# Attention scores of a second dense stage: three products over 64 rows per head instead of two over 128 stacked rows

## The chip, the cores and the metric

One Trainium2 chip, one NeuronCore. The metric is the device time of one execution in microseconds (us), the median of several runs. TensorE (PE in the profile; PEld are its weight loads), VectorE (DVE), ScalarE (ACT), GpSimd (POOL) and SyncE (SP) work side by side, each through its own queue in order.

## The reference

Two transformer blocks on one sequence of 1024 tokens of 1024 features, each with a dense part and a mixture of 32 experts. The change lies in the dense part of the second block, which has two kinds of attention, 8 heads of 64 features each:

```python
h = _modulate(_rmsnorm(x, g_mix[layer]), shift_mix, scale_mix)
qkv = h @ w_in[layer]
...
o_dil = _dilated_mixture(heads_d(q_d), heads_d(k_d), heads_d(v_d)).reshape(b, s, D_DIL)
o_sb = _stick_breaking_attention(heads_s(q_s), heads_s(k_s), heads_s(v_s)).reshape(b, s, D_SB)
mixed = jnp.concatenate([_rmsnorm(o_dil, g_dil_out[layer]), _rmsnorm(o_sb, g_sb_out[layer])], axis=-1)
x = x + gate_mix[:, None, :] * (mixed @ w_out[layer])
```

In the first kind the scores `q @ k.T / 8` get a bias by distance and a softmax over all keys up to the query. In the second, `A[t,s] = sigmoid(z_ts) * prod_{s<j<t} (1 - sigmoid(z_tj))` with the same scores z. In both the weights then multiply the values.

## The kernel before

All is float32. Where precision matters, a product is made of exact parts: each operand is split into a high part (the leading 12 bits) and a low part, in a format that TensorE takes in one pass, and the products high x high, high x low and low x high are summed (`mm3`, lines 108 to 113).

The second dense stage is `dense2` (from line 1241). It norms the eight blocks of 128 tokens, and then works through eight jobs, pairs of heads: four of the first kind (`kind` 0), then four of the second. For each pair, `pair_qkv` (line 1328) makes keys, queries and values of 1024 tokens with `gemm` (line 284; 24 products of 512 columns for each half of the tokens and each of the three), and `pair` (line 1346) does the attention. `pair_qkv` of the next pair is issued after `pair` of this one. The order on each engine is set by a scheduler at build time, which interleaves them: dense products of the next pair lie between the scores, transposes and outputs of this pair. At run time each engine keeps to that order.

The keys and queries come out of `gemm` with the two heads in the two halves of the 128 partitions. `put_q` (line 302) writes for each head a tile `qs` of 128 partitions: 64 with the high part, 64 with the low part. `put_k` (line 312) writes for each head a tile `kh` that holds the high part twice and a tile `kl` that holds the low part twice; the second copy is made by GpSimd (line 321). So a head's scores are two products over all 128 rows, `qs` with `kh` and `qs` with `kl` (`scores`, line 335; lines 345 and 346). Keys up to the end of the query block are taken in one cut of up to 512, or in two equal cuts when there are more; a cut fills a PSUM buffer `sc`, of which there are three.

`pair` goes through eight blocks of 128 queries and in each through two heads `j`. Kind 0: VectorE adds the bias from a table `tb` and takes the maximum (line 1368), ScalarE takes the exponential, VectorE normalises into `s`. Kind 1: ScalarE takes the sigmoid into `be` (line 1380), GpSimd zeroes what lies after the query (line 1381), `ke` is one minus that, VectorE runs a product scan into `s` (line 1389) and multiplies. Then TensorE transposes the weights (`tp`, line 1399), ScalarE copies them to `pT`, and the output `po` takes both heads alternately in the two halves of its partitions (line 1404). That product has 64 columns of weights: a tile shape of 128 rows x 64 columns, against 128 x 128 for everything around it.

When the first kind is done, `half_out` (line 1300) multiplies its output with half of the output projection: for each of eight row blocks it loads rows of x into one of four buffers `xs`, makes 24 products, scales them into `ys` (VectorE, line 1324), adds (GpSimd, line 1325) and stores to `xp`. In the order its products fill the last pair. `xs` and `ys` take the places of the query and key tiles of the pairs with even number (`qs1`, `kh0`, `kh1`, `kl0`, `kl1`); the pairs with odd number hold theirs in another pool. After the stage `out_proj` (line 748) does the other half of the projection, the router and the experts.

```python
qs, kh, kl = ([new(2 * n + j, f"{m}{j}") for j in range(2)] for n, m in enumerate(("qs", "kh", "kl")))
vt = p.tile([P, NB, P], FT, name="vt", bufs=2)
...
for j in range(2):
    parts = self.scores(pp, qs[j], kh[j], kl[j], qb)
```

Of the kernel before, what the change touches and what calls it, by code (L numbers as in the profile page):

```python
# [8 lines left out]
FT = mybir.dt.float32  # L9
# [3 lines left out]
AF = mybir.ActivationFunctionType  # L13
OP = mybir.AluOpType
# [19 lines left out]
V_AT = 3  # L34
LATE = {1: (2, 3, 5), 2: (2, 3, 4, 5, 6, 7)}


def bcast(ap, n=P):
    """Rows of DRAM read into all partitions."""
    return bass.AP(tensor=ap.tensor, offset=ap.offset, ap=[[0, n]] + [list(a) for a in ap.ap])  # L40


def rev(ap):
    """A [partition, free] view read from its end."""
    step, n = ap.ap[-1]
    return bass.AP(tensor=ap.tensor, offset=ap.offset + step * (n - 1), ap=[list(ap.ap[0]), [-step, n]])
# [5 lines left out]
class Shared:  # L52
    """A pool of which some tags, two tiles each, lie in the tiles that are kept throughout."""
# [11 lines left out]
class Kern:  # L65
# [21 lines left out]
    def held(self, i, shape, dt, name):  # L87
        """One of six tiles of 4 KB that stay in place: weights, then rows of x, then queries and keys."""
        return self.keep.tile(shape, dt, tag=f"k{i}", name=name, bufs=1)

# [1 line left out]
    def later(self, op, first, why, sync=True):  # L92
        """op after the end of first, or, in one queue, after its issue."""
# [4 lines left out]
    def split(self, pool, src, shape, tag, bufs=None, eng=None):  # L98
        """Exact parts of float32: hi has the leading 12 bits, lo the rest."""
# [27 lines left out]
    def ada_first(self, which, p, pp, n):  # L127
        """Shift and scale of the first norm, features on partitions; the first step starts n loads."""
# [49 lines left out]
    def mod_store(self, which, p, r, ps):  # L178
        """Four rows of the modulation: with its bias; for a scale, gain * (1 + it). They go to DRAM,
        the first four (the first shift and scale) stay as sums."""  # L180
# [19 lines left out]
    def mod_cols0(self, which, pp, tag, bufs):  # L200
        """mod_first() from the sums of mod_store()."""
# [7 lines left out]
    def mod_first(self, which, sums):  # L209
        """Per feature (on partitions): scale and shift of the first norm."""  # L210
# [10 lines left out]
    def cond(self, which):  # L221
        """silu(c), features on partitions."""
# [39 lines left out]
    def mod_cols(self, which, pp, tag, j):  # L262
        """Per feature (on partitions): scale and shift from the modulation rows j + 1 and j."""
# [11 lines left out]
    def mod_row(self, pool, which, j, name, after=None, t=None):  # L275
        """Modulation row j on all partitions."""
# [7 lines left out]
    def gemm(self, pp, w, x, evac, halves=(0, 1), after=None):  # L284
        """evac(half, psum) with 128 output features on partitions, 512 tokens."""
# [16 lines left out]
    def put_q(self, qs, half, ps):  # L302
        """Two heads' queries, scaled; each stacked with its own low part."""
# [8 lines left out]
    def put_k(self, kh, kl, half, ps, after=None):  # L312
        """Two heads' keys: high parts, and low parts, each twice."""
# [11 lines left out]
    def put_v(self, pool, pp, vt, half, ps):  # L325
        """Two heads' values, tokens on partitions."""
# [8 lines left out]
    def scores(self, pp, qs, kh, kl, qb):  # L335
        """Scores of a block of queries with all keys up to it: (psum, first key, keys)."""
        nc = self.nc
        n = (qb + 1) * P
        cuts = [(0, n)] if n <= 512 else [(0, n // 2), (n // 2, n)]
        got = []  # L340
        for c0, c1 in cuts:
            sc = pp.tile([P, 512], FT, tag="sc", name="sc", bufs=3)
            o = sc[:, :c1 - c0]
            q = qs[:, qb * P:(qb + 1) * P]
            nc.tensor.matmul(o, q, kh[:, c0:c1], start=True, stop=False)
            nc.tensor.matmul(o, q, kl[:, c0:c1], start=False, stop=True)
            got.append((o, c0, c1 - c0))
        return got

# [1 line left out]
    def t5_flag(self, ahead):  # L351
        """Biases for positions that don't rise by one, where needed. Returns a register: 0, or 1
        where they were. ahead() starts the loads that needn't wait for it."""
# [1249 lines left out]
```

## Time and profile before

| | |
|---|---|
| time, median of 3 runs | 2549.51 us (2544.28 to 2554.2) |
| profiled execution: span from the first to the last instruction | 2542.7 us (its own time is not listed; 6.8 us less than the median of the runs) |
| busy share of the span: PE, DVE, ACT, POOL | 89%, 65%, 25%, 16% |
| second dense stage, first score to last output | 1318.7 to about 1892 us |
| output projection, router | about 1899 to 2000 us |
| experts of the second block | about 2000 to 2498 us |

The page of the profile gives one execution. Busy times count the time from an instruction's start to its end; on TensorE the next product starts well before the last one's end, so the distance of starts says more than the duration. Idle time is put down to what released the instruction after it; "issue" means that nothing the profile shows released it.

### The profile page before, as it was taken

To read this page: it belongs to the slowest core of one execution; us is meant where nothing else is said; L and a number is where in the kernel's file an instruction comes from. 1 tells how busy PE (TensorE), PEld (TensorE's weight loads), DVE (VectorE), ACT (ScalarE), POOL (GpSimd) and SP (SyncE) were. 2 spreads that over 40 slices of the span, in tenths; PEclk is the share of its full clock that TensorE was granted. 3 is DMA by queue.
4 is the path that set the end of the run, shared out by engine and by line. 5 is a ranking of instruction groups with operands and counts; after the bars stand their busy time and mean duration, and the time that the engine had idled before them with its cause. 6 is when DMAs were issued, how large, how long until landed. Compare 5 with 4: busy or idle time off the path is not lost. (4 is left out here: it accounts for less than half of the span.)

```text
span 2542.7 us, 55236 instructions
## 1 busy us (share of the span) xinstructions
PE 2258.6 (89%) x23070; PEld 1634.2 (64%) x23070; DVE 1664.2 (65%) x3712; ACT 646.3 (25%) x1406; POOL 415.1 (16%) x509
## 2 busy tenths in 40 slices
PE   7999999999969999979389999999989699999761
PEld 4777767687847655646267777777668476655530
DVE  4565678724787777766365555667868877776535
ACT  4455211111310000000155455555543100000001
POOL 2101012113220000000230100222342200000002
PEclk9999999999979999999689999999999799999986
DMA  7232477727569999998831111000547799999997
GB/s 275 84 96 63 137 264 242 240 74 261 193 253 424 424 422 423 381 414 365 356 124 55 34 50 34 26 30 18 179 165 292 279 424 423 423 418 382 426 424 291
DMA packets 112125, 628.38 MB, mean 247 GB/s; under 512 B 16025, under 2 KB 33018, under 8 KB 86522
## 3 DMA queue, kind: packets, MB, share of 16 engines
q1 hardware_dynamic: 92592, 574.96, 57.9%
q0 software_dynamic: 17312, 48.35, 4.9%
q8 instruction: 185, 3.03, 0.5%
q10 hardware_dynamic: 1962, 1.44, 0.2%
q14 instruction: 74, 0.61, 0.1%
HBM read 579.57 MB, written 55.61 MB: 250 GB/s over the span
## 5 line engine op out<-in xcount | busy, mean ns | idle before, releaser
L888 PE MATMUL ps<-gu,xT 128*32 128x256 f32 x10368 | 635.1, 389 | 51.2 <-DMA gu<-in_w_up_dram 37.8
L888 PEld LDWEIGHTS ps<-gu,xT 128*32 128x32 f32 x10368 | 392.6, 113 | 260.4 <-issue 69.5
L903 DVE TENSOR_TENSOR yq<-py,g 32x256 f32<-32x256 f32 x648 | 271.9, 420 | 176.0 <-PE py L899 131.6
L899 PE MATMUL py<-dn,hT 128*32 128x256 f32 x5184 | 332.4, 390 | 50.2 <-DVE hT L895 48.7
L110 PE MATMUL mm<-hh,gh 128*128 128x512 f32 x864 | 347.3, 403 | 4.8 <-ACT hh L1451 3.5
L111 PE MATMUL mm<-hl,gh 128*128 128x512 f32 x864 | 345.0, 399 | 0.4 <-DVE hl L1475 0.4
L112 PE MATMUL mm<-hh,gl 128*128 128x512 f32 x864 | 344.1, 398 | 0.0
L883 DVE STREAM_TRANSPOSE xT<-xg 32x256 f32<-32x256 f32 x648 | 282.1, 435 | 70.6 <-PE ps L888 60.0
L899 PEld LDWEIGHTS py<-dn,hT 128*32 128x32 f32 x5184 | 184.9, 112 | 164.0 <-DVE hT L895 82.1
L891 ACT ACTIVATE sg<-ps 128x128 f32<-128x128 f32 x162 | 44.7, 277 | 913.1 <-PE ps L888 905.0
L110 PEld LDWEIGHTS mm<-hh,gh 128*128 128x128 f32 x864 | 162.9, 189 | 48.1 <-ACT sg L517 5.2
L112 PEld LDWEIGHTS mm<-hh,gl 128*128 128x128 f32 x864 | 163.0, 189 | 37.0 <-issue 0.9
L111 PEld LDWEIGHTS mm<-hl,gh 128*128 128x128 f32 x864 | 163.2, 189 | 36.5 <-issue 1.0
L912 POOL DMA_INDIRECT s_y<-yq,sx x39 | 38.9, 996 | 606.9 <-DVE yq L903 564.5
L169 DVE SCALAR_TENSOR_TENSOR acc<-wa,cs,acc 128x512 f32<-128x512 f32 x140 | 110.1, 791 | 36.0 <-DMA wa<-in_w_ada_dram 33.2
L105 DVE TENSOR_TENSOR gl<-graw,gh 128x1024 fp32r<-128x1024 f32 x61 | 80.9, 1326 | 65.5 <-ACT gh L104 64.0
L104 ACT ACTIVATE gh<-graw 128x1024 fp32r<-128x1024 f32 x66 | 69.9, 1059 | 197.2 <-PE mm L111 176.7
L893 DVE TENSOR_TENSOR hm<-sg,ps 128x128 f32<-128x128 f32 x162 | 64.0, 396 | 74.7 <-ACT sg L891 70.2
L1400 ACT ACTIVATE pT<-tp 128x512 f32<-128x512 f32 (+2 forms) x192 | 90.1, 491 | 85.3 <-PE tp L1399 84.4
L1389 DVE TENSOR_TENSOR_SCAN s<-ke 128x128 f32<-128x128 f32 (+7 forms) x64 | 92.3, 1444 | 21.0 <-ACT ke L1385 19.8
L1404 PE MATMUL po<-pT,vt 128*64 128x128 f32 x1152 | 103.2, 282 | 1.9 <-ACT pT L1400 1.8
L1404 PEld LDWEIGHTS po<-pT,vt 128*64 128x64 f32 x1152 | 70.7, 136 | 38.3 <-issue 25.1
(377 smaller groups left out, 3220.8 us busy)
## 6 DMA issues: line engine op xcount, KB each, us to landing
gu<-in_w_gate_dram SPq DMA_DIRECT2D x62, 2048.0 KB, 18.7
gu<-in_w_up_dram SPq DMA_DIRECT2D x62, 2048.0 KB, 22.2
dn<-in_w_down_dram SPq DMA_DIRECT2D x62, 2048.0 KB, 23.6
wa<-in_w_ada_dram SPq DMA_DIRECT2D x96, 512.0 KB, 5.0
graw<-in_w_in_dram SPq DMA_DIRECT2D x54, 512.0 KB, 3.6
cy<-s_y SPq DMA_DIRECT2D x32, 512.0 KB, 6.7
bt<-s_t5all SPq DMA_DIRECT2D x32, 256.0 KB, 2.8
s_hp<-rh SPq DMA_DIRECT2D x16, 512.0 KB, 2.9
```

The lines of the kernel that those rows point to most:

```text
L105: (eng or nc.vector).tensor_sub(lo, src, hi.bitcast(FT))
L110: o = nc.tensor.matmul(ps, lh, rh, start=first, stop=False)
L111: nc.tensor.matmul(ps, lh, rl, start=False, stop=False)
L112: nc.tensor.matmul(ps, ll, rh, start=False, stop=last)
L169: nc.vector.scalar_tensor_tensor(acc, wt[:, k], c, acc, op0=OP.mult, op1=OP.add)
L883: turn = V.transpose(out=xT[32 * q:32 * q + 32].rearrange("p k t -> p (k t)"), in_=xg[o, 256 * q:256 * q + 256])
L888: mm = nc.tensor.matmul(ps[32 * q:32 * q + 32], xT[:, k, :], gu[:, :, k, q * P:(q + 1) * P], start=(k == 0), stop=(k == KD - 1))
L899: nc.tensor.matmul(py[32 * q:32 * q + 32], hT[:, k, :], dn[:, k, 256 * q:256 * q + 256], start=(k == 0), stop=(k == 3))
L903: V.tensor_mul(yq[o, 256 * q:256 * q + 256], py[r], g2[r])
L1389: V.tensor_tensor_scan(out=rev(s[:, :n]), data0=rev(ke[:, :n]), data1=rev(ke[:, :n]), initial=1.0, op0=OP.mult, op1=OP.bypass)
L1400: nc.scalar.activation(pT[:, 4 * g:4 * g + m], pt[:, :m], AF.Copy)
L1404: nc.tensor.matmul(po[64 * j:64 * j + 64, :], vt[:, kb, 64 * j:64 * j + 64], pTs[j][:, kb, :], start=(kb == 0), stop=(kb == qb))
```

## The change

The scores of the second dense stage are made of three products over the 64 rows of a head, high x high, low key, low query, for both heads in turn: head 0 in rows 0 to 63, head 1 in rows 64 to 127, each into a buffer `sc` of its own. Keys and queries are kept as four tiles of both heads (`qh`, `ql`, `kh`, `kl`), written by `put_parts` in full height; nothing is copied. `pair` takes the scores of both heads, cut by cut, before it goes on with each head. Buffers: `s` 4 instead of 3, `st` 6 instead of 3, the tag `u` (`tb`, `be`, `ke`) 5 instead of 4. `half_out` has fewer tiles to take over, so its fourth `xs` and its `ys` take the two tiles of `vt`. The order that kept the first pair's copies behind the norm goes with the copies. The first block's own attention (`sliding`) keeps `put_q` and `put_k`. The change also drops docstrings and comments; code lines move down by up to 14.

```diff
+    def put_parts(self, hi, lo, half, ps, scale=1.0):
+        nc = self.nc
+        s = slice(half * 512, half * 512 + 512)
+        nc.scalar.activation(hi[:, s], ps, AF.Copy, scale=scale)
+        nc.vector.scalar_tensor_tensor(lo[:, s], ps, scale, hi[:, s].bitcast(FT), op0=OP.mult, op1=OP.subtract)
+
-    def scores(self, pp, qs, kh, kl, qb):
+    def scores(self, pp, held, qb):
         nc = self.nc
+        qh, ql, kh, kl = held[:4]
         n = (qb + 1) * P
-        cuts = [(0, n)] if n <= 512 else [(0, n // 2), (n // 2, n)]
-        got = []
-        for c0, c1 in cuts:
-            sc = pp.tile([P, 512], FT, tag="sc", name="sc", bufs=3)
-            o = sc[:, :c1 - c0]
-            q = qs[:, qb * P:(qb + 1) * P]
-            nc.tensor.matmul(o, q, kh[:, c0:c1], start=True, stop=False)
-            nc.tensor.matmul(o, q, kl[:, c0:c1], start=False, stop=True)
-            got.append((o, c0, c1 - c0))
-        return got
+        t = slice(qb * P, (qb + 1) * P)
+        for c0, c1 in [(0, n)] if n <= 512 else [(0, n // 2), (n // 2, n)]:
+            sc = [pp.tile([P, 512], FT, tag="sc", name="sc", bufs=3)[:, :c1 - c0] for j in range(2)]
+            for m, (q, k) in enumerate(((qh, kh), (qh, kl), (ql, kh))):
+                for j in range(2):
+                    r = slice(64 * j, 64 * j + 64)
+                    nc.tensor.matmul(sc[j], q[r, t], k[r, c0:c1], start=(m == 0), stop=(m == 2))
+            yield c0, c1 - c0, sc
...
-        g1 = qp.tile([P, D], FT, tag="qs0", name="g1", bufs=1)
+        g1 = qp.tile([P, D], FT, tag="qh", name="g1", bufs=1)
...
-        xs = [qp.tile([P, D], FT, tag=t, name="xs", bufs=1) for t in ("qs1", "kh0", "kh1", "kl0")]
-        ys = qp.tile([P, 2, 512], FT, tag="kl1", name="ys", bufs=1)
+        xs = [qp.tile([P, D], FT, tag=t, name="xs", bufs=1) for t in ("ql", "kh", "kl")] + [qp.tile([P, D], FT, tag="vt", name="xs", bufs=2)]
+        ys = qp.tile([P, 2, 512], FT, tag="vt", name="ys", bufs=2)
...
-        qs, kh, kl = ([new(2 * n + j, f"{m}{j}") for j in range(2)] for n, m in enumerate(("qs", "kh", "kl")))
+        qh, ql, kh, kl = (new(n, m) for n, m in enumerate(("qh", "ql", "kh", "kl")))
...
-        puts = (lambda half, ps: self.put_k(kh, kl, half, ps, after),
-                lambda half, ps: self.put_q(qs, half, ps),
+        puts = (lambda half, ps: self.put_parts(kh, kl, half, ps),
+                lambda half, ps: self.put_parts(qh, ql, half, ps, 0.125),
...
+            ss_ = [p.tile([P, T + 1], FT, name="s", bufs=4) for j in range(2)]
...
+            for m, (k0, c, sc) in enumerate(self.scores(pp, held, qb)):
+                for j in range(2):
+                    if kind == 0:
+                        V.tensor_tensor_reduce(ss_[j][:, k0:k0 + c], sc[j],
+                                               tb[j][:, T - n + k0:T - n + k0 + c], 1.0, NEG, OP.add, OP.max,
+                                               sts[j][:, m:m + 1])
+                    else:
+                        nc.scalar.activation(bes[j][:, k0:k0 + c], sc[j], AF.Sigmoid)
             for j in range(2):
-                parts = self.scores(pp, qs[j], kh[j], kl[j], qb)
-                s = p.tile([P, T + 1], FT, name="s", bufs=3)
+                s = ss_[j]
```

The order on the engines changes with it. First place: TensorE, first pair of the stage, around the end of the sixth query block (`sc`, `tp`, `po` are scores, transposes and outputs, `mm` dense products; numbers tell tiles apart). Before:

```order
L1404 MATMUL po_14273<-pT_14301,vt_13969 64x128
L1399 MATMUL tp_14341<-ident_58,s_14325 128x128
L345 MATMUL sc_14407<-kh1_13966,qs1_13964 128x384
L346 MATMUL sc_14407<-kl1_13968,qs1_13964 128x384
L345 MATMUL sc_14410<-kh1_13966,qs1_13964 128x384
L346 MATMUL sc_14410<-kl1_13968,qs1_13964 128x384
L1399 MATMUL tp_14360<-ident_58,s_14350 128x128 x4
L345 MATMUL sc_14447<-kh0_13965,qs0_13963 128x448
L346 MATMUL sc_14447<-kl0_13967,qs0_13963 128x448
L112 MATMUL mm_14753<-hh_13617,gl_14616 128x512
```

Now:

```order
L1418 MATMUL po_14261<-pT_14291,vt_13967 64x128
L1413 MATMUL tp_14345<-ident_58,s_14309 128x128
L355 MATMUL sc_14390<-kh_13965,qh_13963 128x384
L355 MATMUL sc_14390<-kl_13966,qh_13963 128x384
L1413 MATMUL tp_14354<-ident_58,s_14310 128x128 x4
L355 MATMUL sc_14390<-kh_13965,ql_13964 128x384
L355 MATMUL sc_14449<-kh_13965,qh_13963 128x448
L355 MATMUL sc_14450<-kh_13965,qh_13963 128x448
L355 MATMUL sc_14449<-kl_13966,qh_13963 128x448
L355 MATMUL sc_14450<-kl_13966,qh_13963 128x448
L355 MATMUL sc_14449<-kh_13965,ql_13964 128x448
L355 MATMUL sc_14450<-kh_13965,ql_13964 128x448
```

`sc_14390` is head 1 alone, its products broken by transposes; `sc_14449` and `sc_14450` are both heads in turn. In the stage as a whole the 576 score products now form 130 groups without another product between; 280 of the 576 stand in 140 pairs of both heads, 296 next to none of the other head. The tile shape changes 283 times from product to product before, and 501 times now.

Second place: TensorE at the end of the last pair (`gh` and `gl` are the parts of the first mixture's output, so `mm<-wo,gh` are products of `half_out`; `mh` is the same for `out_proj`). Before:

```order
L1404 MATMUL po<-pT,vt 64x128 x15
L1414 MATMUL pq<-sq,ones 32x256 x4
L1424 MATMUL pc<-ident,sums 128x4 x2
L270 MATMUL mcps<-ident,mcm 128x16
L110 MATMUL mm<-wo,mh 128x512
```

Now:

```order
L1418 MATMUL po<-pT,vt 64x128 x15
L1428 MATMUL pq<-sq,ones 32x256 x4
L1438 MATMUL pc<-ident,sums 128x4 x2
L111 MATMUL mm<-wo,gh 128x512
L112 MATMUL mm<-wo,gh 128x512
L113 MATMUL mm<-wo,gl 128x512
```

72 products of `half_out`, three row blocks of it, now stand after the last output, ahead of `out_proj`.

Third place: the loads of `half_out`'s rows on SP (`xs_19304` and `xs_19352` are the fourth buffer; in brackets the queues that a load waits for). Before:

```order
L1316 DMA xs_19302<-s_x2 128x1024 [waits PE_49,Pool_49]
L1316 DMA xs_19304<-s_x2 128x1024 [waits PE_49,Pool_49]
L1310 DMA graw_19376<-s_oT 128x4x256 [waits DMAHW1_49,DVE_49]
L1316 DMA xs_19303<-s_x2 128x1024 [waits PE_49,Pool_49]
L1316 DMA xs_19301<-s_x2 128x1024 [waits PE_49]
```

Now:

```order
L1324 DMA xs_19350<-s_x2 128x1024 [waits DMASW4_49,Pool_49]
L1324 DMA xs_19351<-s_x2 128x1024 [waits DMASW5_49,Pool_49]
L816 DMA xn_19866<-s_xp 128x1024 [waits PE_49]
L1324 DMA xs_19352<-s_x2 128x1024 [waits PE_49]
L280 DMA g1_19676<-s_mod2 128x1024 [waits DMAHW3_49,DVE_49]
```

The fourth buffer's first load stood among the first loads; now it stands behind the second round of two others. It lies at the address of the last pair's `vt`, which the last outputs read.

## Rows read from the trace of the kernel before

**Rows 1.** Stretches of the stage: length, busy us (PE PEld DVE ACT POOL), clock, DMA.

```profile
1318.70:1600.00 281.30, 278.79 (x1703) 216.97 (x1701) 152.86 (x478) 144.72 (x313) 30.26 (x47) 1.00 0.13 43
1600.00:1890.00 290.00, 278.59 (x1767) 213.43 (x1765) 213.60 (x304) 156.27 (x308) 93.60 (x119) 0.99 0.22 75
```

**Rows 2.** Timeline of TensorE, 1505.3 to 1507.9 us: start, us, product, partitions x columns.

```profile
1505.66 0.34 PE L346 MATMUL sc<-kl,qs 128*128 128x384 f32 x1
1505.84 0.40 PE L111 MATMUL mm<-hl,gh 128*128 128x512 f32 x1
1506.07 0.39 PE L112 MATMUL mm<-hh,gl 128*128 128x512 f32 x1
...
1506.54 0.60 PE L1399 MATMUL tp<-ident,s 128*128 128x128 f32 x4
```

**Rows 3.** TensorE by line, 1318.7 to 1890 us: count | busy, mean ns | idle; then line 345.

```profile
L110 PE MATMUL mm<-hh,gh 128*128 128x512 f32 x356 | 144.3, 406 | 0.0
...
L1404 PE MATMUL po<-pT,vt 128*64 128x128 f32 x1122 | 101.2, 282 | 1.9 <-ACT pT L1400 1.8
...
L1399 PE MATMUL tp<-ident,be 128*128 128x128 f32 x288 | 48.3, 283 | 5.6 <-ACT pT L1400 3.0 <-DVE be L1391 1.4 <-DVE s L1388 1.1
...
L110 PE MATMUL mm<-wo,gh 128*128 128x512 f32 x64 | 26.6, 415 | 2.4 <-ACT gh L104 2.0 <-DVE ys L1324 0.4
...
L345 PE MATMUL sc<-kh,qs x192: 221/369/506, 1319.0 to 1876.7; 128*128 128x384 f32 x48, 128*128 128x512 f32 x48, 128*128 128x320 f32 x32, 128*128 128x448 f32 x32
```

**Rows 4.** Timeline of TensorE around a visit to the output shape.

```profile
1503.32 0.42 PE L346 MATMUL sc<-kl,qs 128*128 128x320 f32 x1
1503.58 0.39 PE L110 MATMUL mm<-hh,gh 128*128 128x512 f32 x1
1503.90 0.87 PE L1404 MATMUL po<-pT,vt 128*64 128x128 f32 x10
1504.70 0.66 PE L1399 MATMUL tp<-ident,s 128*128 128x128 f32 x4
```

**Rows 5.** Waits of the weight loads, 1318 to 1890 us: total us, times, longest.

```profile
PEld po L1404 <- issue: 24.9, 90, 0.4
PEld tp L1399 <- issue: 14.9, 75, 1.5
...
PEld sc L345 <- ACT be L1380: 4.2, 5, 1.4
```

**Rows 6.** Timeline of TensorE around visits to the 64-row shape (line 393).

```profile
24.63 0.61 PE L1438 MATMUL nT<-dg,x 128*128 128x128 f32 x4
...
24.86 0.39 PE L1438 MATMUL nT<-dg,x 128*128 128x128 f32 x2
25.17 0.59 PE L393 MATMUL mm<-oh,rr 33*128 33x384 f32 x1
25.60 0.48 PE L393 MATMUL mm<-oh,rr 33*128 33x384 f32 x1
26.01 0.49 PE L1438 MATMUL nT<-dg,x 128*128 128x128 f32 x2
...
28.42 0.81 PE L393 MATMUL mm<-oh,rr 33*128 33x384 f32 x2
```

**Rows 7.** All engines by line, 1300 to 1910 us: evacuation of queries and keys.

```profile
L321 POOL CAST kh<-kh 64x512 fp32r<-64x512 f32 x32 | 24.5, 764 | 192.3 <-ACT kh L318 191.7
...
L309 DVE SCALAR_TENSOR_TENSOR qs<-mm,qs 64x512 fp32r<-64x512 f32 x32 | 22.0, 688 | 29.2 <-ACT qs L308 28.5
...
L318 ACT ACTIVATE kh<-mm 64x512 fp32r<-64x512 f32 x32 | 18.8, 588 | 12.1 <-PE mm L112 6.2 <-DVE kl L319 3.8 <-DVE s L1388 0.8
```

**Rows 8.** The same view: GpSimd's additions of half_out.

```profile
L1325 POOL TENSOR_TENSOR xs<-xs,ys 128x512 f32<-128x512 f32 x16 | 26.2, 1639 | 21.1 <-DVE ys L1324 18.2 <-DVE s L1388 2.9
```

**Rows 9.** Timeline of TensorE from the last outputs to the projection.

```profile
1890.19 1.96 PE L1404 MATMUL po<-pT,vt 128*64 128x128 f32 x30
...
1899.01 0.79 PE L110 MATMUL mm<-wo,mh 128*128 128x512 f32 x1 [3.35 <-ACT mh L736]
```

More of the change, by code (lines that the diff above doesn't have):

```diff
@@ L34 @@
 V_AT = 3
+NU = 5
 LATE = {1: (2, 3, 5), 2: (2, 3, 4, 5, 6, 7)}
@@ L1273, in dense2 @@
         pp = st["a"].enter_context(self.pool("atps", 1, psum=True))
-        held = self.pair_qkv(qp, pp, wp, gp, hh, hl, *jobs[0], self.root, ws)
+        held = self.pair_qkv(qp, pp, wp, gp, hh, hl, *jobs[0], ws)
         for n, (kind, i) in enumerate(jobs):
@@ L1326, in half_out, with pair_qkv @@
                 nc.gpsimd.dma_start(xp[t, :], xt)
-    def pair_qkv(self, p, pp, wp, gp, hh, hl, kind, i, after=None, ws=None):
+    def pair_qkv(self, p, pp, wp, gp, hh, hl, kind, i, ws=None):
         a = self.a
@@ L1343, in pair_qkv @@
                 self.gemm(gp, w, (hh, hl), put, halves)
-        return qs, kh, kl, vt
+        return qh, ql, kh, kl, vt
     def pair(self, p, pp, held, kind, i, o_dram, ss):
@@ L1349, in pair @@
         V = nc.vector
-        qs, kh, kl, vt = held
+        vt = held[4]
         oT = p.tile([P, T], FT, name="oT", bufs=1)
@@ L1354, in pair @@
             for j in range(2):
-                t = p.tile([P, T], FT, tag="u", name="tb", bufs=4)
+                t = p.tile([P, T], FT, tag="u", name="tb", bufs=NU)
                 nc.sync.dma_start(t, a["dil"][2 * i + j])
@@ L1361, in pair @@
             pTs = []
+            ss_ = [p.tile([P, T + 1], FT, name="s", bufs=4) for j in range(2)]
+            if kind == 0:
+                sts = [p.tile([P, 6], FT, name="st", bufs=6) for j in range(2)]
+            else:
+                bes = [p.tile([P, T], FT, tag="u", name="be", bufs=NU) for j in range(2)]
+            for m, (k0, c, sc) in enumerate(self.scores(pp, held, qb)):
+                for j in range(2):
+                    if kind == 0:
+                        V.tensor_tensor_reduce(ss_[j][:, k0:k0 + c], sc[j],
+                                               tb[j][:, T - n + k0:T - n + k0 + c], 1.0, NEG, OP.add, OP.max,
+                                               sts[j][:, m:m + 1])
+                    else:
+                        nc.scalar.activation(bes[j][:, k0:k0 + c], sc[j], AF.Sigmoid)
             for j in range(2):
-                parts = self.scores(pp, qs[j], kh[j], kl[j], qb)
-                s = p.tile([P, T + 1], FT, name="s", bufs=3)
+                s = ss_[j]
                 if kind == 0:
-                    st = p.tile([P, 6], FT, name="st", bufs=3)
-                    for m, (o, k0, c) in enumerate(parts):
-                        V.tensor_tensor_reduce(s[:, k0:k0 + c], o,
-                                               tb[j][:, T - n + k0:T - n + k0 + c], 1.0, NEG, OP.add, OP.max,
-                                               st[:, m:m + 1])
-                    if len(parts) == 2:
+                    st = sts[j]
+                    if n > 512:
                         V.tensor_max(st[:, 0:1], st[:, 0:1], st[:, 1:2])
@@ L1377, in pair @@
                 else:
-                    be = p.tile([P, T], FT, tag="u", name="be", bufs=4)
-                    for o, k0, c in parts:
-                        nc.scalar.activation(be[:, k0:k0 + c], o, AF.Sigmoid)
+                    be = bes[j]
                     nc.gpsimd.affine_select(be[:, n - P:n], be[:, n - P:n], pattern=[[-1, P]], base=-1,
                                             channel_multiplier=1, compare_op=OP.is_ge, fill=0.0)
-                    ke = p.tile([P, T], FT, tag="u", name="ke", bufs=4)
+                    ke = p.tile([P, T], FT, tag="u", name="ke", bufs=NU)
                     if qb > 4:
@@ L1409, in pair @@
                 nc.gpsimd.dma_start(o_dram[:, s], oT[:, s])
-        sq = p.tile([P, T + 1], FT, tag="s", name="sq", bufs=3)
+        sq = p.tile([P, T + 1], FT, tag="s", name="sq", bufs=4)
         nc.scalar.activation(sq[:, :T], oT, AF.Square)
```

## The prediction

> **What bounds the kernel now.** I read the granted clock first (1.00 in nearly all of the stage), then the stretches of the second dense stage, then the spacing of single TensorE products. From 1318.7 to 1890 us TensorE is busy for 278.8 of 281.3 us and 278.6 of 290.0 us, while VectorE is busy for 153 and 214 us and ScalarE for 145 and 156 us [rows 1]. Busy time overstates TensorE, because its products overlap, so I went to the starts. A product of 512 columns on all 128 rows follows its forerunner after 0.23 us, one of 384 columns after 0.18 us [rows 2]: 0.455 ns a column. A transpose of 128 columns follows after 0.11 us: four span 0.60 us, and one alone lasts about 0.27 [rows 2].
>
> With these spacings the stage can be added up from its counts [rows 3]. The dense products are 3 x 357 and 3 x 64 of 0.233 us, 294 us. The scores are 384 products; each of the two lines has 48 of 512 and of 384 columns, 32 of 448 and of 320, and by the code 16 of 256 and of 128, that is 73,728 columns, so 147,456 x 0.455 ns = 67.1 us. The transposes are 2 x 288 and 64 in the values, 640 x 0.109 = 70 us. The outputs are 576 products of two passes each (1152 records, of which 1122 lie here); the two heads run side by side in the two halves of the columns, and in the order 237 pairs do so and 102 products stand alone, so 339 x 2 x 0.109 = 74 us, 2 of them after 1890. The sums of squares are 3 us. What is left is changes of tile shape. A product of 128 rows and 64 columns starts 0.32 us after a product of 512 columns instead of 0.23; its first pair takes about 0.05 us longer than the other four; after the last pair (the group from 1503.90 ends at 1504.77, so its last product began at 1504.49) the transposes start 0.21 us later instead of 0.11; and a product in full shape has its first weight load in the open, since 1503.32 to 1503.58 is 0.26 us for 320 columns instead of 0.15 [rows 4]. So 0.145 us to go into the output shape and 0.20 us to go back. The order has 134 changes into it and 141 to full shape: 19.4 + 28.2 = 48 us. The sum is 554 us of 571 us. **TensorE bounds this stage**, its products are dense, and only about 17 us of the stage are waits for others. The trace names the same time in another way: the weight loads sit idle 24.9 us in 90 places before outputs and 14.9 us in 75 before transposes, released by nothing ("issue") [rows 5]. After the stage comes the output projection, also on TensorE, then routing and experts, so a shift of the stage's end is a shift of the kernel's end.
>
> **The change part by part.** Scores: 384 products on 128 rows become 576 on 64 rows. If the two halves of the rows run at once, two products that stand side by side cost one slot. In the order that was built only 140 such pairs stand side by side (54,400 columns); 296 products of one head stand alone (114,624 columns), because three score buffers hold one cut of both heads and half of the next. That is 169,024 x 0.455 ns = 76.9 us against 67.1: **+9.8 us**. With every pair side by side it would be 110,592 columns, 50.3 us; with no overlap at all 221,184 columns, 100.6 us. The trace shows tiles running at once for column halves only (five pairs of outputs in 0.59 us from first to last start, [rows 4]), so overlap of row halves is taken from the nearest row, and 100.6 us stays as the other end. Each half also has its own weight load; where two loads queued (0.107 us each, the delays of first loads in [rows 4, 6]) the pairs would be load-bound below 470 columns, +5.8 us. In [rows 4] loads of column halves go side by side, so I take 0 and keep 5.8 as the end.
>
> The rows do show one packing that bears on this: pairs of column halves take 0.109 us, no longer than one product. The Trainium skill's page "TensorE: Matmul & The Clock Gate" (Part 3, measured speedup) has four row tiles at 3.07 times instead of 4. By that the 24.8 us of pairs would be 32.3 us and the sum 7.5 us higher; no run here shows it, and the sum goes by the row.
>
> Tile shape: this is the large term. The shape of 64 rows occurs in the trace, in eight products early in the kernel [rows 6]. In full shape products of 128 columns are 0.11 us apart there (four span 0.61 us, two 0.39), so the last one before a visit starts at 24.97; the 64-row product starts 0.20 us later instead of 0.11; the next one 0.43 us later, where two in steady state are 0.33 apart; the way back takes 0.41 instead of 0.32; and the second full product starts at 26.22 (its group ends at 26.50, one lasts 0.28), 0.21 instead of 0.11. So 0.20 us in and 0.19 us out: 0.198 a change. In the old order scores are in full shape and run on between transposes and dense products. In the new order there are 129 changes into the 64-row shape, 229 to full shape instead of 141, and 135 into the output shape instead of 134: 217 more at 0.198 us, **+43.0 us**. Bound from below: 0, if all were hidden in waits; the row that it is nearest to is that of [rows 6], the same shape, with the same cost in each of its visits.
>
> Evacuation: 64 copies on GpSimd go (24.5 us for the 32 of `kh`, about as much for `kl`), VectorE's 64 half-height steps become 32 of full height (0.69 us each, 22 us less), ScalarE the same (0.59 us, 19 us less) [rows 7]. None of this is on TensorE; it shortens what TensorE waits for, of which there are 17 us. Bounds 0 and 17; I take half, **-8 us**: VectorE and ScalarE lose only about 6% of their time, but TensorE's own queue gets longer, so that they are late less often.
>
> The end of the stage: `half_out` takes the two tiles of values as its fourth row buffer and its product buffer; the fourth, `xs`, is the last pair's, so its load waits on SP for the last output product. Behind it on SP stand the gate row, late rows and mixture loads of the output projection; on GpSimd the additions of five row blocks; and 72 dense products (16.8 us) now come after the last output. Ten additions of 1.64 us [rows 8] take 16.4 us beside them. Today 6.9 us pass from the last output (1892.15) to the projection's first product (1899.01) [rows 9]; then some 23 us will, of which 16.8 are work that has moved. That is 6 us without work, as today: **0**. The other end is 16 us, if none of the additions had work beside it; nearest is today's gap, since the 72 products need no more than the two buffers that they have now.
>
> Sum: 9.8 + 43.0 - 8 + 0 = **+45 us**. The profiled span is 2542.7 us; the page gives no own time for it. The median of three runs is 2549.5, so 6.8 us lie around the span and stay. Forecast 2549.5 + 45 = 2594.5 us.
>
> **The rivals.** (1) Not slower: the changes of shape cost little, since TensorE's queue is not always the last to be ready. Its place is the 130 visits to the 64-row shape. It decides below (17 - 9.8) / 217 = 0.033 us a change with every wait returned. At 0 the sum is 9.8 - 17 = -7, 2542 us; at 0.033 us it is no change, 2549.5 us. For it: eight products only show the shape. Against it: all visits show 0.20, and output visits, over a hundred, show the same. (2) The halves of the rows do not run at once: scores 100.6 instead of 76.9 us, +23.7, 2618 us. For it: no row shows row halves. (3) A new wait: both heads take two of three score buffers, so each second cut waits until VectorE or ScalarE has drained one. TensorE's loads wait today 5 times, 4.2 us, for that (`sc` behind `be`) [rows 5]. At 0.84 us for each of the 32 query blocks that have two cuts, +27, 2621 us. (4) That the heads do not alternate at all places is no rival but in the sum, from the order.
>
> **How the numbers follow.** Half a per cent (13 us) is about what a measurement can tell from no change. Forecast 0.66, rival 1 0.14, rival 2 0.11, rival 3 0.09. The forecast's own range is 2585 (all 17 us of waits returned: +36) to 2624 (none returned, 5.8 of queued loads, 16 at the end: +75). The range takes in rivals 2 and 3 and, downward, changes at a little over half their price (0.11 us: 9.8 + 23.9 - 8 = +26, 2575): 2570 to 2621. It leaves out rival 1 and little more. Faster (below 2536.8): 0.03, the part of rival 1 in which work off TensorE counts for more than the sum shows. Same (to 2562): the rest of rival 1 and 0.02 of the forecast, 0.13. Slower: 0.84.
>
> **What would show it.** Right: in the new profile the scores of two heads on 64 rows start within some 10 ns of each other where they stand side by side; idle time of weight loads by "issue" in the stage about doubles (50 to 90 us); the stretch from the first score to the last output grows by some 25 to 35 us and the rest lies in the 72 products behind it; GpSimd's share falls. Wrong: a 64-row visit that costs under 0.1 us each way; the second of two neighbours a whole slot later (rival 2); waits of scores for `be` or `st` of over 20 us (rival 3); a stage that ends earlier although "issue" grew, which would say that the waits, not the products, had set its length.

## The result, and the profile after

The changed kernel takes 2584.53 us (median of 4 runs, 2582.95 to 2585.8), the kernel before 2551.59 us in the same comparison (2544.28 to 2554.2): a ratio of 1.014, 95% interval 1.0118 to 1.0163. It is 33 us slower, inside the range given, and on the side that was forecast. The profiled executions differ by 41.4 us in span (2584.1 and 2542.7): 3.8 us of it ahead of the first score, 35.7 from there to the projection, 1.8 after it. In the changed kernel 1.7 us lie around the span (2585.8 us for the profiled run); by that the profiled run of before was its fastest, 2544.28 us, and the 6.8 us that I had put around its span are mostly the scatter of the runs.

The stretches that answer to [rows 1], in the changed kernel (columns as there):

```profile
1322.80:1600.00 277.20, 276.92 (x1684) 199.52 (x1684) 129.34 (x432) 126.72 (x277) 3.96 (x7) 1.00 0.12 40
1600.00:1906.00 306.00, 303.28 (x1917) 214.47 (x1917) 201.67 (x313) 159.19 (x313) 60.28 (x83) 1.00 0.17 56
```

GpSimd falls from 30 and 94 us to 4 and 60 (about 16 us of this are ten additions that now stand behind the last output), VectorE by 24 and 12, ScalarE by 15 in sum, and TensorE is now busy in all but 3.0 us of 583. The work was taken off engines that were not the bound.

Weight loads of the stage by what ended their idle time (total us, times, longest), against [rows 5]:

```profile
PEld po L1418 <- issue: 25.8, 93, 0.4
PEld sc L355 <- issue: 19.3, 93, 0.4
PEld tp L1413 <- issue: 15.8, 89, 0.4
PEld mm L111 <- issue: 10.0, 35, 0.4
PEld mm L113 <- issue: 8.0, 35, 0.4
...
PEld mm L112 <- issue: 7.0, 26, 0.4
...
PEld sc L355 <- ACT be L1382: 1.5, 5, 0.4
...
PEld sc L355 <- DVE st L1378: 1.4, 5, 0.4
```

Two groups are much larger than before: the loads of the scores, and those of the dense products that follow a visit to the 64-row shape. In the kernel before they were:

```profile
PEld sc L345 <- issue: 3.9, 17, 0.7
...
PEld mm L110 <- issue: 2.1, 12, 0.2
```

Scores hardly wait for a buffer: 1.5 us for `be` and 1.4 for `st`. TensorE's timeline shows one visit with one head and one with both (start, us, product):

```profile
1505.10 0.39 PE L112 MATMUL mm<-hl,gh 128*128 128x512 f32 x1
1505.42 0.41 PE L355 MATMUL sc<-kh,qh 64*128 64x320 f32 x1
1505.67 0.30 PE L355 MATMUL sc<-kl,qh 64*128 64x320 f32 x1
1505.82 0.31 PE L355 MATMUL sc<-kh,ql 64*128 64x320 f32 x1
1506.05 0.50 PE L113 MATMUL mm<-hh,gl 128*128 128x512 f32 x1
1506.39 0.40 PE L111 MATMUL mm<-hh,gh 128*128 128x512 f32 x1
1506.63 0.39 PE L112 MATMUL mm<-hl,gh 128*128 128x512 f32 x1
...
1509.15 0.41 PE L355 MATMUL sc<-kh,qh 64*128 64x320 f32 x2
1509.40 0.31 PE L355 MATMUL sc<-kl,qh 64*128 64x320 f32 x2
1509.55 0.31 PE L355 MATMUL sc<-kh,ql 64*128 64x320 f32 x2
1509.79 0.50 PE L113 MATMUL mm<-hh,gl 128*128 128x512 f32 x1
```

Into the shape: 0.32 us instead of 0.23 to the first score, then 0.25 instead of 0.15 to the second. Out of it: 0.23 instead of 0.15, then 0.34 instead of 0.23. That is 0.19 us each way. The visit with both heads does twice the work and takes 0.64 us from first score to dense product, the one with a single head 0.63. So the halves of the rows do run at once.

To see the whole stage this way I took the starts of all TensorE products from the first score to the last output, and split each distance to the next start into four parts. A **slot** is the usual spacing, fitted to these traces: 6 + 0.4435 N ns for a dense or score product of N columns (0.233 us for 512), 0.109 us for a transpose or one pass of an output product; two that start within 25 ns share one. A **change** is what goes beyond it at a change of shape and at the product after (up to 0.200 and 0.125 us). A **wait** is any more than that. A small rest (irregular spacings, and heads that overlap without being neighbours; at most 8 us) is left out below, so that the parts do not quite add up to the stretch.

Changes and waits separate well, because a change costs nearly the same everywhere. In the changed kernel the distance at a change exceeds the slot by 0.09 us in the median, and nine in ten stand within 0.08 and 0.105. The next distance adds 0.10 us where the new shape's products are dense or scores, and 0.05 to 0.06 where they are outputs or transposes. What is booked as change above these medians adds up to 4.4 us, against 1.9 in the kernel before.

Each row is one execution. From the projection to the end, where the code is the same, the executions with the reference's scores take 641.9 to 647.2 us, so a difference of some 5 us between two rows says little. All kernels of this study, in us:

| kernel | first score to last output | slots | changes: count, us | waits | last output to projection | median of runs |
|---|---|---|---|---|---|---|
| before | 572.9 | 508.1 | 281, 44.3 | 27.1 | 7.1 | 2551.6 |
| after | 583.3 | 496.9 | 500, 86.1 | 7.5 | 32.5 | 2584.5 |
| e1_tail | 599.0 | 513.7 | 495, 85.4 | 7.2 | 4.2 | 2575.8 |
| e2_two_full | 551.9 | 487.3 | 281, 43.6 | 26.7 | 31.8 | - |
| e3_joint1 | 582.5 | 469.4 | 381, 69.7 | 44.0 | 31.3 | 2584.7 |
| e4_joint2 | 650.1 | 475.8 | 402, 75.8 | 97.5 | 31.5 | 2649.0 |
| e5_three_full | 585.0 | 522.0 | 281, 45.6 | 24.1 | 31.7 | 2584.6 |
| e6_headwise | 586.3 | 499.5 | 508, 87.2 | 7.2 | 30.8 | 2588.2 |
| e7_two_full_tail | 567.6 | 504.4 | 279, 42.8 | 26.4 | 6.9 | - |
| e8_three_plain | 592.1 | 539.1 | 277, 42.3 | 18.0 | 3.7 | - |
| e9_one_visit | 560.6 | 497.0 | 141, 21.5 | 48.2 | 4.1 | 2530.8 |
| e10_pairs | 552.9 | 497.0 | 181, 28.3 | 35.2 | 6.8 | 2523.4 |
| e11_full_outputs | 585.0 | 559.8 | 14, 2.2 | 28.1 | 6.6 | 2554.6 |
| e12_change_pairs | 583.6 | 504.5 | 405, 71.7 | 14.2 | 3.7 | 2556.8 |

Where the 72 products of the half projection (16.8 us) stand behind the last output, they count in the last stretch and not in the first. That is so in after and in e2 to e6. Runs without a median had scores that are not the reference's, so their totals cannot be compared. The counts of changes in other places of this text run over slightly longer stretches.

From the first score to the first product of the projection the change adds 615.8 - 580.1 = **35.7 us**: 219 more changes of shape 41.8 us; scores 4.6 (76.6 - 67.7 = 8.9 of slots, less 4.3 where the two heads overlap without being neighbours); waits -19.6; the end +8.6 (32.5 - 16.8 - 7.1); 12 dense products that now stand ahead of the first score -2.8; irregular spacings +3.1.

The end, by stretches (length, busy us of PE PEld DVE ACT POOL, clock, DMA), and what SP's queue waited for there:

```profile
1906.00:1909.00 3.00, 1.00 (x14) 0.28 (x11) 0.42 (x1) 1.33 (x2) 0.56 (x1) 0.99 0.53 147
1909.00:1912.60 3.60, 1.02 (x4) 0.93 (x4) 1.07 (x3) 0.00 (x0) 2.02 (x2) 0.50 0.95 298
1912.60:1915.40 2.80, 2.73 (x6) 2.15 (x7) 0.77 (x2) 0.00 (x0) 2.61 (x5) 0.50 0.40 117
1915.40:1930.50 15.10, 15.10 (x65) 12.17 (x64) 3.75 (x5) 0.00 (x0) 11.03 (x10) 0.99 0.74 240
1930.50:1938.60 8.10, 0.88 (x5) 0.33 (x3) 1.02 (x4) 0.63 (x1) 1.92 (x3) 0.86 0.71 234
```

```profile
SPq L816 <- DMA s_xp<-xs: 18.9, 4, 6.5
SPq L1324 <- PE po L1418: 12.9, 1, 12.9
```

There are two holes where there was one. Apart from the sums of squares TensorE stands idle until 1912.67. The load of the fourth `xs` was issued only after the last output; GpSimd's addition waits for it, VectorE's `ys` for the addition, and the next dense product for `ys`. TensorE starts again at a granted clock of 0.50 (the 1.2 GHz level of its two). Then it runs through the 72 products and, from about 1931, stands idle once more, because the projection's features (`fore`) are loaded behind the rows `xn` on SP, and those wait for the stores of `xp`. The wait of the addition, and then the queues in order of time:

```profile
POOL xs L1333 <- DMA xs<-s_x: 3.0, 1, 3.0
```

```profile
1906.39 0.32 SPq L1324 DMA_DIRECT2D xs<-s_x  x1
...
1912.67 0.80 PE L111 MATMUL mm<-wo,gh 128*128 128x512 f32 x1 [2.66 <-DVE ys L1332]
...
1933.30 0.39 SPq L782 DMA_DIRECT2D fore<-s_oT  x1
...
1938.59 0.79 PE L111 MATMUL mm<-wo,mh 128*128 128x512 f32 x1 [6.31 <-ACT mh L744]
```

### The profile page after: what moved, and what is told of

Read it like the earlier page. It is cut to its first block, busy times and chain, and to the rows that moved or that the text cites. A ratio compares the mean times of both kernels' runs of the same rounds, so it can differ in the third digit from the quotient of the medians.

```text
span 2584.1 us, 55403 instructions
## 1 busy us (share of the span) xinstructions
PE 2303.1 (89%) x23262; PEld 1629.0 (63%) x23262; DVE 1634.9 (63%) x3680; ACT 628.4 (24%) x1372; POOL 362.8 (14%) x445
```

## The experiments

**e1_tail: the end alone.**

```diff
-xs = [... for t in ("ql", "kh", "kl")] + [qp.tile([P, D], FT, tag="vt", name="xs", bufs=2)]
-ys = qp.tile([P, 2, 512], FT, tag="vt", name="ys", bufs=2)
+xs = [... for t in ("ql", "kh", "kl")] + [self.held(4, [P, D], FT, "xs")]
+ys = self.held(5, [P, 2, 512], FT, "ys")
```

> The changed kernel, with the fourth row tile and the product tile of the half projection in two kept tiles that the new score layout leaves free, instead of the tiles of values. In the order as built the 72 products of the half projection stand ahead of the last output again. Theory (the end costs time): the stretch from the last output to the output projection falls from 32.5 us to the 7 us of the kernel before, of which 16.8 us move back ahead of the last output and 8.6 us are gained: 2584.5 - 9 = 2576 us (2571 to 2580). Rival 1 (the end is bound by the additions on GpSimd and the loads on SP in either place): 2583 to 2586 us. Rival 2 (the 72 products also fill waits beside the last pair): a gain of 12 to 18 us, 2567 to 2572.

Measured 2575.8 us (a ratio to the kernel before of 1.0103, 1.0086 to 1.012): 8.7 less than the change. TensorE in its profile, from the last outputs to the projection:

```profile
1918.99 1.96 PE L1418 MATMUL po<-pT,vt 128*64 128x128 f32 x30
...
1924.84 0.80 PE L111 MATMUL mm<-wo,mh 128*128 128x512 f32 x1
```

The 72 products are ahead of the last output again, and the stage with them grows by 15.7 us, nearly their own 16.8: they filled no waits. The end was worth 8.7 us by the medians. The two profiled executions, the fastest of e1 and the slowest of the change, differ by 12.7 us in this stretch.

**e2_two_full: no 64-row shape, two products per head.**

```diff
-for m, (q, k) in enumerate(((qh, kh), (qh, kl), (ql, kh))):
+for m, (q, k) in enumerate(((qh, kh), (ql, kl))):
     for j in range(2):
-        r = slice(64 * j, 64 * j + 64)
-        nc.tensor.matmul(sc[j], q[r, t], k[r, c0:c1], ...)
+        nc.tensor.matmul(sc[j], q[:, t], k[:, c0:c1], ...)
```

> The changed kernel with everything kept but the scores: two products on all 128 rows per head (high query with high key, low query with low key, over the rows of both heads) instead of three on 64 rows; the score values are not the reference's. No visit to the 64-row shape is left, 286 changes of shape in the order instead of 505, and 67.7 us of score columns instead of 77. Theory (shape changes at about 0.2 us are the loss, and the simpler evacuation gave back some 20 us): 219 x 0.205 + 9 = 54 us less, 2531 us, below the kernel before (2525 to 2538). Rival 1 (the changes of shape are cheap, the loss lies in the buffers, the order or the end): 2570 us or more. Rival 2 (the changes cost what was said but the evacuation gave nothing back): 2551 us, the time before.

The routing to the experts follows from the scores and came out otherwise here: the experts took longer, and the total (2837 us) cannot be compared. From first score to projection it is 583.6 us, against 615.8 after and 580.1 before: 32 us less than the change and not 54. The changes go (-42.5), the score slots go (-8.9), but 19.2 us of waits come back. They are what the kernel before had (26.7 and 27.1), although the copies are gone. So the simpler evacuation did not give back 20 us, as the theory had it.

**e3_joint1, e4_joint2: both heads always together.** One tile of two banks for both heads, so that neither can start without the other; one such tile and three transpose buffers, or two and one.

```diff
-sc = [pp.tile([P, 512], FT, tag="sc", name="sc", bufs=3)[:, :c1 - c0] for j in range(2)]
+both = pp.tile([P, 2, 512], FT, tag="sc2", name="sc", bufs=1)
+sc = [both[:, j, :c1 - c0] for j in range(2)]
```

> The changed kernel with the scores of both heads in one tile of two banks (one such tile) and three transpose buffers instead of three single score buffers and two transpose buffers. In the order as built 276 of 288 pairs of score products stand side by side (105,792 columns, 24 products alone) and there are 386 changes of shape instead of 505. Theory (shape changes at 0.2 us and unpaired halves are the loss): 119 x 0.205 = 24 us and 77 - 53 = 24 us less, 2536 us, below the kernel before, if the single tile brings no wait. Rival (the next cut waits until both heads of the cut before are drained, about 1.3 us and a detour for each of the 96 cuts, hidden in part): a third of them exposed is +40 us, 2576 us; all of them would be over 2620 us.

> As the run before, but two score tiles of two banks and one transpose buffer. In the order as built 280 pairs stand side by side and there are 407 changes of shape. Theory: 98 x 0.205 = 20 us and 25 us less than the changed kernel, 2539 us, if one transpose buffer brings no wait. Rival: each of the 96 query rows of a head with a second group of transposes waits for the drain of the first (0.60 us and its way on ScalarE): +60 us or more, 2600 us.

2584.65 and 2649.03 us. In e3 changes and score slots cost 40 us less than in the change (16.4 and 23.6), and 36.5 us of waits eat it. What TensorE waited for in e3 (us, times, longest):

```profile
PE tp L1415 <- DVE be L1407: 14.6, 10, 3.7
PE sc L356 <- ACT be L1384: 4.6, 4, 1.8
PE sc L356 <- DVE st L1380: 3.3, 4, 1.7
```

and in e4:

```profile
PE tp L1415 <- ACT pT L1416: 52.8, 67, 3.7
```

In e3 scores wait for the drain of both heads. Transposes wait for weights, probably because their scores came late; no line shows that step. The pairs can be had; the price seems to be the third buffer, which let the next head begin. With one transpose buffer many second groups wait for the drain of the first, as the rival said, but e4 came out 49 us above the rival's 2600.

**e5_three_full: the change's arithmetic in full shape.** Two tiles of queries for each head, zero in the other head's rows, by a scale per row. The heads also come one after the other, the query steps on ScalarE and VectorE double, and `u` and `s` are back to 4 and 3 buffers, for space.

```diff
+self.rows = ...  # per row: 0.125 in the head's 64 rows, 0 elsewhere
-self.put_parts(qh, ql, half, ps, 0.125)
+[self.put_parts(qh[j], ql[j], half, ps, self.rows[j]) for j in range(2)]
...
-nc.tensor.matmul(sc[j], q[r, t], k[r, c0:c1], ...)
+nc.tensor.matmul(sc[j], q[j][:, t], k[:, c0:c1], ...)
```

> The changed kernel with its three products per head on all 128 rows: each head has its own queries, zero in the rows of the other head, so that no 64-row shape is left and the scores are the same sums. 286 changes of shape instead of 505, but 101.6 us of score columns instead of 77.6. Theory (a change costs about 0.21 us wherever it stands): 46 us less and 24 us more, 2562 us, up to 16 us more if the waits that the longer TensorE queue had covered come back: 2558 to 2578. Rival (changes of shape are cheap, the loss lies elsewhere): 24 us more, 2608 us.

2584.64 us, the change's own time, and 6.6 us above the theory's upper edge. The profile has both terms: changes 40.5 us less, score slots 25.0 more, 4.3 of overlap lost. The 11 us that this leaves went into waits, which grew by 16.6, most of what the change had covered. So the times agree by accident, not because changes are free: with free changes the rival's 2608 us would have been due. Some of the waits may come from the fewer buffers and the doubled query steps; no run separates these.

**e6_headwise: the heads one after the other.**

```diff
-for m, (q, k) in ...:
-    for j in range(2):
+for j in range(2):
+    for m, (q, k) in ...:
```

> The changed kernel with the three products of the first head issued ahead of the three of the second, instead of alternately. In the order as built 80 pairs stand side by side instead of 140, 416 products alone instead of 296 (88.6 us of slots instead of 77.6), and 513 changes instead of 505. Theory (row halves run at once only where they are neighbours): 11 + 2 = 13 us more, 2597 us (2591 to 2601). Rival (the alternation is worth nothing, because the halves overlap anyway or never do): 2584 to 2587.

2588.2 us: 3.6 more, not 13, and 1 us above the rival's range. At 1361.17 the queue holds three products of head 0 and then three of head 1:

```profile
1361.17 0.42 PE L355 MATMUL sc<-kh,qh 64*128 64x320 f32 x2
1361.42 0.32 PE L355 MATMUL sc<-kl,qh 64*128 64x320 f32 x2
1361.57 0.31 PE L355 MATMUL sc<-kh,ql 64*128 64x320 f32 x2
1361.81 0.50 PE L112 MATMUL mm<-hl,gh 128*128 128x512 f32 x1
```

Three pairs all the same. In all 33 visits with this order the other head's first product starts 10 ns after the first one's, two products ahead of its turn. Alternation is not what makes the halves run at once; having both heads in one visit is.

**e7_two_full_tail, e8_three_plain: are the copies or the queue what moves the waits?** e7 is e2 with the tiles of e1; e8 makes three products on all rows for each head, one head after the other. Each ran once.

> The second run (two products per head on all 128 rows, scores not the reference's) with the free tiles of the first run at the end. TensorE then does in the stage what it does in the kernel before (284 changes of shape, 67.7 us of score columns), but the 64 copies on GpSimd and the half-height steps are gone. Only the stretch from the first score to the first product of the output projection is compared (580.1 us before), since routing depends on the scores. Theory (the copies were hidden): 576 to 584 us. Rival (the simpler evacuation gives back the waits of TensorE, some 20 us): 558 to 565 us.

> The run before with a third product per head on all 128 rows (queries of both heads in one tile, so the scores are not the reference's): 33.9 us more of score columns on TensorE, 282 changes of shape, nothing else added. The same stretch is compared. Theory (work added to TensorE first fills its waits): the stretch grows by 15 to 22 us against the run before, and the waits of TensorE beyond the usual spacings fall from some 20 us to under 8. Rival (the waits follow from dependences and stay): it grows by 32 to 35 us.

e7: 574.5 us (1325.3 to 1899.8), 5.6 less than before and just past the theory's edge. Of this 2.8 are dense products that stand ahead of the first score, and the rest is within what two executions differ by. Waits are 26.4 us against 27.1: without copies and half-height steps TensorE waits as long as with them. The copies were hidden. And with neither the 64-row shape nor the late end, nothing of the change's 35.7 us is left. e8: 595.8 us, 21.3 more, for 34.7 us more slots: waits fall by 8.4, the end by 3.2. The theory's growth held; that waits would fall below 8 us did not (18.0).

**e9 to e11: the same prices on the outputs of the kernel before.** The outputs are the stage's other change of shape. e9 holds them, by one added dependence, until both heads' weights are transposed; e10 does so per group of four key blocks:

```diff
+if j == 0 and kb == 0:           # e10: kb % 4 == 0, that group's last drain
+    self.later(op, lasts[-1], "both heads")
```

e11 takes the shape away: each head, one after the other, against the values of both heads, its 64 rows kept.

```diff
-nc.tensor.matmul(po[64 * j:64 * j + 64, :], vt[:, kb, 64 * j:64 * j + 64], pTs[j][:, kb, :], ...)
+nc.tensor.matmul(po[:, j, :], vt[:, kb, :], pTs[j][:, kb, :], ...)
```

> The kernel before (its own score layout), with the outputs of a query block held until both heads' weights are transposed: all 288 pairs of output products stand side by side (237 pairs and 102 products alone before) in 64 visits instead of 134. 146 changes of shape in the order instead of 286. Theory (changes of shape and unpaired halves are time on TensorE wherever they stand, some 0.16 us a change with its first load, 0.218 us an output slot): 140 x 0.157 = 22 us and 51 x 0.218 = 11 us less, of which the run with three full products suggests that about half comes back as waits: 2533 us (2518 to 2545), faster than both kernels. Rival (outputs so late bring a wait of their own on the one output buffer and at the end of each pair): 2550 us or more.

> As the run before, but held for each group of four key blocks instead of the whole query block: 288 pairs side by side in 84 visits, 186 changes of shape. Theory: 100 x 0.157 = 16 us and 11 us less, about half of it back as waits: 2537 us (2523 to 2548). Against the run before it tells whether the fewer visits or the earlier start of outputs counts for more. Rival: 2550 us or more.

> The kernel before, with its outputs on all 128 columns: each head's weights against the values of both heads, into its own half of a bank, of which the head's 64 rows are kept. 19 changes of shape instead of 286, but 576 slots of 0.218 us instead of 339. Theory: 267 x 0.157 = 42 us less and 52 us more, +10 us, part of it in waits that are there already: 2555 us (2549 to 2562). Rival (a change costs more than its gap shows, because the queue behind it stands still too): clearly faster, under 2540 us.

e9 2530.8 us (0.9925, 0.9901 to 0.9948), **e10 2523.4 us (0.9903, 0.9865 to 0.9942)**, e11 2554.6 us (1.0027, 1.0012 to 1.0041). All three are within 14 us of the number expected and inside the ranges. e9 and e10 beat both kernels. e9 saves more in changes (22.8 us against 16.0) and the same 11.1 in slots, but 21.1 us come back as waits against 8.1. In e9 scores wait 7.5 us for `be` (2.6 in the kernel before) and transposes 5.3 us for `pT` (3.3 before), so the later outputs bring waits of their own. That outputs held for a group can start earlier is the likely reason why e10 has fewer; no run shows it by itself, and the intervals of e9 and e10 overlap. In e11 42.1 us of changes pay for most of 51.7 us of slots.

**e12_change_pairs: e10's outputs in the changed kernel, with e1's tiles.**

> The changed kernel with the free tiles of the first run at the end and the held outputs of the run with 84 visits: 288 pairs of outputs side by side, 410 changes of shape in the order instead of 505 (the best old layout has 186). Theory: against the first run 90 x 0.17 = 15 us and 11 us less, of which little comes back, since TensorE's queue is long here (7 us of waits): 2575.8 - 22 = 2554 us (2549 to 2562); the 64-row layout then still loses some 30 us to the old one with the same outputs (2523), by 224 changes of shape. Rival (with the outputs held the two layouts cost the same): 2530 us or less.

2556.8 us (1.0038, 1.0018 to 1.0057). With the better outputs and the end mended the 64-row layout is still 33 us behind the old one: 224 changes more, 43.4 us, and 7.5 us more of slots; against this stand 21 us of waits that the old one has and this one has not.

## Why the prediction was right, step by step

The mechanism was right: the work that the change saves lies on engines that were not the bound, and what it costs is changes of tile shape on TensorE, at the price that was read from the rows. The number also owes something to terms that miss in opposite directions. The time lies 0.5 us under the forecast's own range (2585 to 2624). The stated range holds it through its lower arm, which was meant for changes at a little over half their price; they came at the full price, and it was the waits that were too small.

**Tile shape, +43.0: right, 41.8.** Eight products early in the kernel [rows 6] gave 0.198 us a change; the 219 that came were worth 0.191 each. (The counts given add up to 218 changes, not 217.) Rival 1 falls with this: e2, e9 and e11 took changes away, and by the split they were worth 0.16 to 0.19 us each. The sign that was named for it was weak: the weight loads' idle time by "issue" was to reach 50 to 90 us and did reach 88.7, but by the same groups it was 49.7 us before, where I had added up two of them (39.8). The Trainium skill's page "TensorEngine Tiling (Array Packing)", Key Properties, says that a change of tiling mode drains TensorE, and gives no price. The trace agrees as far as it shows: the first product after a change starts 0.09 us late. The other half of the price lies in that product's weight load, which starts only with the product itself. After the visit above, the dense product at 1506.05 lasts 0.50 us instead of 0.40; the next one's load starts 0.23 us ahead of it:

```profile
1506.05 0.19 PEld L113 LDWEIGHTS mm<-hh,gl 128*128 128x128 f32 x1 [0.19 <-issue]
1506.16 0.19 PEld L111 LDWEIGHTS mm<-hh,gh 128*128 128x128 f32 x1
```

**Scores, +9.8: 4.6.** The halves run at once, so rival 2 falls. I counted as pairs only products that are neighbours in the order; e6 shows that a head's products also start ahead of their turn, so visits such as three of one head and three of the other cost three slots and not five. (The ten passes of outputs in [rows 4] are four pairs and one product alone, not five pairs; that they overlap stands.)

**Waits, -8: -19.6, and the reason was wrong.** I put them down to lighter evacuation, "VectorE and ScalarE lose only about 6% of their time", and named the longer queue beside it. What came back is more than the bound of 17: my sum over the stage left 17 us for waits, and the split finds 27.1. One reason is that it put all ways back from the output shape at 0.20 us, while 89 of them lead to transposes and cost 0.15. e2 and e7 have the light evacuation and the old waits. e2 differs from the change in the scores alone, and in the order built from them, and its waits are 19.2 us longer. So they were covered by the longer work of the 64-row scores on TensorE. More work alone does not explain it: with 34.7 us more of slots than e7, e8 waits 8.4 us less, and e5, with as much more than e2 (but fewer buffers), only 2.6 less. Why changes of shape cover more than slots do is open.

**The end, 0: +8.6.** The step that failed here is "That is 6 us without work, as today". I saw the load behind the last output, the additions, and the loads that stand behind it on SP, but not that the rows among these wait for the additions' stores, and the projection's features behind them. So the end holds two idle stretches, and TensorE leaves both at the lower clock; before it was one. The term lay inside the bound of 16.

**The sum, +45: +33 in medians, +35.7 in the profiled stretch.** Too high by the waits (11.6) and the scores (5.2), too low by the end (8.6). One sign was set wrongly: the stretch from first score to last output was to grow by 25 to 35 us, but it grew by 10.4, since I had not taken out of it the 16.8 us of products that leave it. Like for like it is 27.2. Rival 3 did not come: scores waited 2.9 us for `be` and `st`. Where the halves were forced together in one buffer (e3) it came in part, with 7.9 us.

## What to carry to other kernels

Ask first which engine's time a change removes: the 64 copies were hidden, and their removal was paid for with 219 changes of tile shape at 0.19 us on the engine that set the end. Where two tile shapes take turns, count visits in the order as built before counting columns; collecting the outputs into fewer, paired visits made the old kernel 1% faster with one added dependence. Work added to an engine that waits now and then costs less than its own time, and work taken from it gives back less: here waits took up a quarter of it (e8) to over a third (e2 against the change). In e9 it is two thirds, but the added dependence brings waits of its own.

## What the runs showed of the hardware that was not expected

Products on different row halves do not keep the order of the queue. With three products of one head ahead of three of the other, the second head's first one starts 10 ns after the first head's first one, in all 33 such visits of e6. I had written that each engine keeps to the order as built; for products on row halves this is not so. The Trainium skill's page "TensorE: Matmul & The Clock Gate" (Part 3, The mechanism) has matmuls start and end strictly in program order; this measurement differs, and it decides. A pair of 64-row products costs one slot to within 0.01 us (0.64 against 0.63 us for a visit). Each half's weight load goes beside the other's: in e6 the two at 1361.17 us start 10 ns apart and together take 0.19 us, and the 5.8 us that I had kept for queued loads did not appear.

```profile
1361.17 0.19 PEld L355 LDWEIGHTS sc<-kh,qh 64*128 64x128 f32 x2 [0.17 <-issue]
```
